# Layer 0 of an encoder trunk: head 3's scores one step later, modulation loaded at three rates, a norm product six tiles wide

## The chip, the cores and the metric

One core of one Trainium2 chip runs the whole kernel in one launch. The metric is the device time of an execution in microseconds. The engines are PE (TensorE: matmuls; its weight loads are shown as PEld), DVE (VectorE), ACT (ScalarE), POOL (GpSimd) and SP (SyncE, which issues the DMAs). SBUF is the memory on the chip from which the engines read; PSUM has eight banks, into which PE writes.

## The reference

A trunk of two layers on 256 tokens of width 2048, in float32. Each layer has two sub-layers, attention and MLP, and each of these is modulated by a conditioning vector `c`:

```python
cond = silu(c)
for l in range(2):
    mod = cond @ w_ada[l] + b_ada[l]                  # 2048 x 12288
    sh_a, sc_a, g_a, sh_m, sc_m, g_m = split(mod, 6)
    h = rmsnorm(x) * (1 + sc_a) + sh_a
    proj = h @ w_in[l]        # dq, dk, dv of 4 differential heads; latent cq, ckv, kr
    out_a = diff_attention(dq, dk, dv, bias)          # softmax(map 0) - lam * softmax(map 1)
    q = rmsnorm(cq) @ w_uq[l]; kv = rmsnorm(ckv) @ w_ukv[l]
    out_b = mla_attention(q, kv, rope(kr))            # 8 latent heads
    x = x + g_a * (concat(out_a, out_b) @ w_o[l])
    h = rmsnorm(x) * (1 + sc_m) + sh_m
    x = x + g_m * (relu(h @ w_mlp_in[l]) ** 2 @ w_mlp_out[l])   # width 8192
return rmsnorm(x) * final_norm_g
```

## The kernel before

**Numbers in two parts.** The weights come from HBM as float32. ACT copies each block to `hi`, which has fewer bits (L144), and DVE makes `lo`, the block less `hi` (L145); the activations are split in the same way. A product is hi x hi + hi x (low activation) + lo x hi. `weights()` does this for one block, 1 MiB as a rule, 0.75 MiB in the norm products. The block lands in a tile `raw`, of which there are five; `hi` and `lo` have four tiles of half a block each, so two blocks' worth.

**Narrow and wide.** `mac` (L177 to L182) issues the three products one by one, each over 256 tokens, and two output tiles share a PSUM bank. `wides` (L191 on) and `wide_by_k` (L248 on) keep a bank for each output tile: the high and the low activations stand side by side, so that one matmul of 512 columns (L201, L258) does the first two products in the two halves of the bank, and one of 256 columns (L204, L260) adds the third. The two halves of the bank have then to be joined: `joined` (an ACT copy, L979, and a DVE add, L980, for each half of a pair of tiles), or `update_wide`, which adds both halves to `x` (L973).

**The modulation.** `w_ada` is 192 blocks of 1 MiB that PE never sees: for each, `ada_load` issues a DMA into one of the five `raw` tiles, and `ada_sums` (L322) has DVE multiply it by `cond` and sum. They are spread over the kernel by credit: every call of `weights()` first queues the sums of what was loaded by the call before, then adds `self.rate` to `self.credit` and issues as many loads as there are whole units in it. `ada_need` forces loads that are wanted at once. The rate before is 0.0 up to the end of layer 0's first norm product, then `RATE_A0` = 1.1 until the MLP's norm product, `RATE_K` = 0.6 in that, and `RATE_M` = 0.66 in the MLP; layer 1 has 0.0, 0.5, 0.7, 0.0 and 0.66. The order of the blocks follows use: shift and scale of the attention's norm, its gate (16 blocks), shift and scale of the MLP's norm (32), the MLP's gate (16), then layer 1.

**The order of a layer** (`layer`, L773). First the norm and the first product; then the rest of `w_d`, the key `w_kr`, and six single columns of `w_t`, with the scores and softmax of the differential heads 0 to 2 (`probs`, `diff_probs`: two maps of two matmuls each, L1036; a DVE reduction, L1037; an exponential on ACT, L1023) between them. Then the latent heads' products up from the latents: keys (`up_k`), four tiles of queries (`up_q(0)`), the rotary part (`up_r`), values (`up_v`), four more tiles of queries (`up_q(1)`), all in PSUM tiles `pss` or `pv`. `probs(3)` stands behind `up_k`. `turn` transposes a head's probabilities. Eight blocks of value weights (`val`, `w_dv`) follow, with the latent heads' scores, transposes and values (`mla`) put between them, then four blocks of `w_oa` (four output tiles by k-quarters) with the differential heads' values (`av`), and twelve tiles of `w_ob` in pairs, each with the update of `x` and its square.

**The MLP's norm product** (`norm_then_by_k`, L660). For each of eight pairs of k-tiles, the normed and modulated pair is made (`modulated`) and multiplied at once, so that the product starts before the norm is through. Six PSUM banks are open. Layer 0 multiplies twelve output tiles narrowly (two to a bank, two weight blocks of 0.75 MiB for each pair), layer 1 six tiles widely (one block for each pair). The tiles of the first 16 that are left, four in layer 0 and ten in layer 1, are made by `wides` in pairs behind it.

The program's own order within an engine is what a scheduler makes of this order when the kernel is built; each engine then works its list from the front.

Of the kernel before, what the change touches and what calls it, by code (L numbers as in the profile page):

```python
# [19 lines left out]
NK = D // P  # L20
# [75 lines left out]
WHOLE = 6  # L96


RATE_A0, RATE_A1, RATE_A2, RATE_K, RATE_K1, RATE_M = 1.1, 0.5, 0.7, 0.6, 0.0, 0.66
FILL = "0|1|2|3||||rlm"  # L100


class Trunk:
# [555 lines left out]

    def norm_then_by_k(self, l, acc, sh, sc, src):  # L660


        r = self.rstd(acc, D, True)
        banks = self.open_banks(6)
        h = []
        for p in range(8):
            k = 2 * p
            for g in (sh, sc):
                self.ada_need(l, g, k + 1)
            new, ins = self.modulated(r, k, self.mod[l, sh], self.mod[l, sc])  # L670
            h += new
            self.hold = None if p else ins
            blocks = self.by_k_weights([src[p, b] for b in range(2 - l)], 6, False)
            if l == 0:
                self.by_k(banks, blocks, h, k, NK, 6)
            else:
                self.wide_by_k(banks, blocks, h, k, NK)
            self.hold = None
        return h, banks

# [92 lines left out]
    def layer(self, l, acc):  # L773
        nc, io = self.nc, self.io
# [15 lines left out]
        if l == 0:  # L790
            early = {p: next_by_k(kqs) for p, kqs in EARLY.items()}
            h, banks = self.first_norm_then_by_k(acc, io["w_a"], 3, fill, early)
        else:
            self.rate = RATE_K1
            h, banks = self.norm_then_by_k(l, acc, 0, 1, io["w_a1"])
        done = sum(len(k) for k in EARLY.values()) if l == 0 else 0
        self.rate = RATE_A0 if l == 0 else RATE_A1
# [25 lines left out]
        def up_k():  # L823
            kn.extend(self.copy(ps, "kn") for ps in self.small(io["w_uk"][l], ckv, 8))

        def up_q(b):
            qn.extend(self.copy(ps, "qn", ms) for ps in self.small(io["w_uq"][l, b], cq, 4))
# [23 lines left out]
        def probs(hd):  # L851
            return lambda: a.append(self.diff_probs(l, hd, q[hd], kk[hd]))
# [28 lines left out]
        if l:  # L881
            self.rate = RATE_A2
        up_k()
        probs(3)()
        up_q(0)
        turn(0)()
        up_r()
        turn(1)()
# [6 lines left out]
        turn(3)()  # L895
        for f in mla[3:6]:
            f()
        self.interleave(
            [val(cg, kq) for cg in range(2) for kq in range(4)],
            mla[6:] + [av[0][0], av[1][0]],  # L900
        )
        acc = None
        g = self.mod[l, 2]
        self.ada_need(l, 2, NK - 1)
        banks = self.open_banks(2)
        self.by_k(banks, self.by_k_weights([io["w_oa"][l, 0]], 4, None), self.mo, 0, NK)
        for f in (av[0][1], av[1][1], av[2][0], av[3][0]):
# [4 lines left out]
        o = self.mo + o  # L912
        for kq in (2, 3):
            self.by_k(banks, self.by_k_weights([io["w_oa"][l, kq]], 4, None), o, 4 * kq, NK)
        for m in range(0, NK, 2):
            if m < 4:
                self.update(m, banks[m // 2], g)
            else:
                self.update_wide(m, self.wides([io["w_ob"][l, m - 4 + j] for j in range(2)], o), g)
            acc = self.sumsq(acc, self.x[:, m : m + 2], m == NK - 2)  # L920

        self.rate = RATE_K1 if l else RATE_K
        h, banks = self.norm_then_by_k(l, acc, 3, 4, io["w_m0"] if l == 0 else io["w_m01"])
        self.rate = RATE_M
        g = self.mod[l, 5]
        acc = None
        late = []
        for fb in range(NFB):
            hid = []
            done = 12 - 6 * l  # L930
            for m in range(0 if fb else done, NK, 2):
                srcs = [io[f"w_m1{l}"][NK * fb + m + j - done] for j in range(2)]
                ps = self.wides(srcs, h)
                if l:
                    banks = [self.joined(banks[i : i + 2], self.t("sum")) for i in range(0, len(banks), 2)]
                for b in banks:
                    hid += self.relu2(b)
                banks = []
                hid += self.relu2(self.joined(ps, self.t("sum")))
            if late:  # L940
                self.ada_need(l, 5, NK - 1)
                for m in range(0, NK, 2):
                    self.update(m, late[m // 2], g)
                late = []
            for m in range(0, NK, 2):
                ps = self.wides([io["w_m2"][l, fb, m + j] for j in range(2)], hid)
                if l == 0 and fb == 0:
# [201 lines left out]
def _layout(i):  # L1149
    f = {k: np.asarray(v) for k, v in i.items()}  # L1150
    a = {}
    a["x"] = np.ascontiguousarray(f["x"][0].reshape(2, P, D))
    a["ck"] = np.ascontiguousarray(f["c"].reshape(NK, P).T)
    pos = f["positions"][0]
    order = [j + 4 * t for j in range(4) for t in range(2)]
    posq = np.tile(pos.reshape(8, 32).T, (4, 1))[:, order]
    a["pos"] = np.ascontiguousarray(np.concatenate([np.broadcast_to(pos, (P, T)), posq], 1))
    a["consts"] = consts()
    feat = lambda v, n: v.reshape(n, P).T
    vec = [feat(f["b_ada"][l], 96) for l in range(2)]  # L1160
    vec += [feat(f["diff_subln_g"][l], 2) for l in range(2)]
    vec += [feat(f["q_norm_g"][l], 4) for l in range(2)]
    vec += [feat(f["kv_norm_g"][l], 2) for l in range(2)]
    vec += [feat(f["final_norm_g"], NK)]
    vec += [np.stack([f[f"diff_lambda_{a}{j}"][l] for a in "qk" for l in range(2) for j in (1, 2)], 1)]
    vec += [np.repeat(f["rel_bias_table"].reshape(8, 4, HD).transpose(1, 0, 2).reshape(4, 32), 32, 0)]
    a["vec"] = np.ascontiguousarray(np.concatenate(vec, 1))
    assert a["vec"].shape == (P, NVEC)
    a["w_ada"] = np.ascontiguousarray(f["w_ada"].transpose(0, 2, 1)).reshape(2, 96, P, D)
    keep = {k: [] for k in ("w_d", "w_t", "w_kr", "w_dv", "w_uq", "w_uk", "w_uv", "w_oa", "w_ob", "w_m2")}  # L1170
    for l in range(2):
        w = f["w_in"][l]
        first = np.concatenate([w[:, 3072:3840], w[:, :768]], 1)
        if l == 0:
            a["w_a"] = np.stack([_kquarters(np.ascontiguousarray(first[:, 768 * j : 768 * j + 768]), 768, 2) for j in range(2)], 1)
        else:
            a["w_a1"] = _kquarters(np.ascontiguousarray(first[:, :768]), 768, 2)[:, None]
            a["w_q1"] = _ktiles(np.ascontiguousarray(first[:, 768:]))
        keep["w_t"].append(_ktiles(np.ascontiguousarray(w[:, 1280:2048])))
        keep["w_d"].append(_kquarters(np.concatenate([w[:, 1024:1280], w[:, 768:1024]], 1)))  # L1180
        keep["w_kr"].append(_ktiles(np.concatenate([w[:, 3840:3904], w[:, 3872:3904], w[:, 3840:3872]], 1))[0])
        keep["w_dv"].append(np.stack([_kquarters(w[:, 2048 + 512 * g : 2560 + 512 * g]) for g in range(2)]))
        w = f["w_uq"][l].reshape(512, HM, 192)
        nope, rope = w[:, :, :128].reshape(512, 1024), w[:, :, 128:].reshape(512, 512)
        keep["w_uq"].append(np.concatenate([_kquarters(np.ascontiguousarray(z)) for z in (nope[:, :512], nope[:, 512:], rope)]))
        w = f["w_ukv"][l].reshape(256, HM, 256)
        keep["w_uk"].append(_kquarters(np.ascontiguousarray(w[:, :, :128]).reshape(256, 1024), 1024, 2)[0])
        keep["w_uv"].append(_kquarters(np.ascontiguousarray(w[:, :, 128:]).reshape(256, 1024), 1024, 2)[0])
        w = np.concatenate([f["w_o"][l][1024:], f["w_o"][l][:1024]])
        keep["w_oa"].append(_kquarters(np.ascontiguousarray(w[:, :512])))  # L1190
        keep["w_ob"].append(_ktiles(np.ascontiguousarray(w[:, 512:])))
        w = f["w_mlp_in"][l]
        if l == 0:
            a["w_m0"] = np.stack([_kquarters(np.ascontiguousarray(w[:, 768 * j : 768 * j + 768]), 768, 2) for j in range(2)], 1)
        else:
            a["w_m01"] = _kquarters(np.ascontiguousarray(w[:, :768]), 768, 2)[:, None]
        a[f"w_m1{l}"] = _ktiles(np.ascontiguousarray(w[:, 1536 - 768 * l :]))
        keep["w_m2"].append(np.stack([_ktiles(f["w_mlp_out"][l][D * b : D * b + D]) for b in range(NFB)]))
    for k, v in keep.items():
        a[k] = np.stack(v)  # L1200
    return a
# [18 lines left out]
```

## Time and profile before

| What | Value |
|---|---|
| Median of three runs | 2212.98 us (2211.97 to 2214.62) |
| The profiled execution's own time | 2212.55 us |
| Its span, first to last instruction | 2210.8 us |
| PE busy | 2180.0 us (99%) |
| DVE busy | 1625.5 us (74%) |
| ACT busy | 1136.4 us (51%) |
| Read from HBM | 581.28 MB, 264 GB/s over the span |
| Mean granted clock of TensorE | 0.997 |

Matmuls are pipelined: one that stands with 0.28 us in a timeline starts 0.12 us behind the one ahead of it. The chain of waits shows these distances. A busy time of PE thus covers short gaps; an idle time is stated in brackets behind a row, with what ended it.

### The profile page before, as it was taken

Reading aid. Unit: us, or ns where it says so; the run is one execution under the profiler, and the core shown is the slowest. Engines: PE = TensorE matmul, PEld = TensorE weight load, DVE = VectorE, ACT = ScalarE, POOL = GpSimd, SP = SyncE. Lnnn points to the kernel's source line nnn. Section 1 sums busy time; section 2 is a strip of 40 time slices with the busy share of each in tenths; the row PEclk is TensorE's granted clock in tenths of the full one; section 3 lists DMA queues with packets and bytes.
Section 4 is the critical chain, followed back from the end, with each engine's and each line's share of the span. In section 5 each row is a group of like instructions: output and inputs, shape, how many; then the busy total and the mean of one; then the engine's idle time right before and its main releaser. Section 6 shows DMA issues by size and latency. Waiting matters only on the chain.

```text
span 2210.8 us, 32403 instructions
## 1 busy us (share of the span) xinstructions
PE 2180.0 (99%) x13010; PEld 1948.1 (88%) x13010; DVE 1625.5 (74%) x2273; ACT 1136.4 (51%) x1691; POOL 1.9 (0%) x10
## 2 busy tenths in 40 slices
PE   7999999999999999999999999999999999999998
PEld 6899888998888888888889988988888888888887
DVE  7899779988878888887886876788655555555555
ACT  6555663465464355355444565546535534534553
POOL 0000000000000000000000000000000000000000
PEclk9999999999999999999999999999999999999999
DMA  9988778888878888888867666677655555555552
GB/s 379 415 348 311 265 269 327 316 328 325 322 305 321 305 323 310 318 324 304 316 218 265 248 229 228 236 263 253 240 189 193 184 189 192 188 183 192 188 189 95
DMA packets 85255, 585.49 MB, mean 265 GB/s; under 512 B 9584, under 2 KB 9968, under 8 KB 19440
## 3 DMA queue, kind: packets, MB, share of 16 engines
q1 hardware_dynamic: 85104, 583.42, 71.1%
q8 instruction: 102, 1.67, 0.3%
q14 instruction: 49, 0.40, 0.0%
HBM read 581.28 MB, written 2.10 MB: 264 GB/s over the span
## 4 chain that ended last, share of the span: by engine, by line
PE 93%; DVE 4%; DMA 2%; ACT 1%; issue 1%; SPq 0%; DVEq 0%; ACTq 0%
PE ps L201 43%; PE ps L204 22%; PE pk L244 3%; PE pk L182 2%; PE pk L181 2%; PE pk L180 2%; PE pk L258 2%; DVE ada L322 2%; PE pv L269 1%; PE pv L270 1%; PE pv L271 1%; DMA ada<-in_w_ada 1%; DVE lo L145 1%; PE pk L260 1%; PE ps L181 1%; PE ps L180 1%
## 5 line engine op out<-in xcount | busy, mean ns | idle before, releaser
L145 DVE TENSOR_TENSOR lo<-raw,hi 128x1024 fp32r<-128x1024 f32 (+1 forms) x714 | 843.0, 1194 | 466.9 <-issue 189.0
L144 ACT ACTIVATE hi<-raw 128x1024 fp32r<-128x1024 f32 (+1 forms) x714 | 731.3, 1035 | 690.6 <-PE ps L201 312.5
L201 PE MATMUL ps<-hid,hi 128*128 128x512 f32 x2048 | 477.5, 390 | 0.0
L322 DVE SCALAR_TENSOR_TENSOR ada<-ada,cond 128x2048 f32<-128x2048 f32 x192 | 438.6, 2286 | 13.6 <-DMA ada<-in_w_ada 13.5
L201 PEld LDWEIGHTS ps<-hid,hi 128*128 128x128 f32 x2048 | 379.7, 188 | 78.1 <-DVE hid L174 1.4
L201 PE MATMUL ps<-h,hi 128*128 128x512 f32 x1856 | 431.7, 390 | 0.0
L201 PEld LDWEIGHTS ps<-h,hi 128*128 128x128 f32 x1856 | 344.7, 188 | 69.2
L204 PEld LDWEIGHTS ps<-hid,lo 128*128 128x128 f32 x2048 | 254.2, 192 | 5.0
L204 PE MATMUL ps<-hid,lo 128*128 128x256 f32 x2048 | 255.7, 283 | 0.0
L204 PEld LDWEIGHTS ps<-h,lo 128*128 128x128 f32 x1856 | 230.3, 192 | 4.5
L204 PE MATMUL ps<-h,lo 128*128 128x256 f32 x1856 | 231.7, 283 | 0.0
L973 DVE SCALAR_TENSOR_TENSOR x<-ps,mod,x 128x256 f32<-128x256 f32 x272 | 124.6, 479 | 6.8 <-PE ps L204 6.6
L979 ACT ACTIVATE sum<-ps 128x256 f32<-128x256 f32 x110 | 42.2, 383 | 115.3 <-PE ps L204 115.1
L182 PE MATMUL pk<-h,lo 128*128 128x256 f32 x320 | 90.4, 283 | 0.0
L181 PE MATMUL pk<-h,hi 128*128 128x256 f32 x320 | 90.4, 283 | 0.0
L180 PE MATMUL pk<-h,hi 128*128 128x256 f32 x320 | 90.1, 285 | 0.0
L244 PE MATMUL pk<-hf,w 128*128 128x256 f32 x384 | 83.9, 379 | 0.0
L244 PEld LDWEIGHTS pk<-hf,w 128*128 128x128 f32 x384 | 72.6, 190 | 10.1 <-ACT hf L614 0.4
L174 DVE TENSOR_TENSOR hid<-relu,hid 128x256 fp32r<-128x256 f32 x128 | 48.3, 422 | 44.8 <-ACT hid L173 44.8
L182 PEld LDWEIGHTS pk<-h,lo 128*128 128x128 f32 x320 | 61.4, 192 | 0.2 <-DVE lo L145 0.2
L181 PEld LDWEIGHTS pk<-h,hi 128*128 128x128 f32 x320 | 61.4, 192 | 0.1
L180 PEld LDWEIGHTS pk<-h,hi 128*128 128x128 f32 x320 | 61.0, 192 | 0.1
(229 smaller groups left out, 2387.0 us busy)
## 6 DMA issues: line engine op xcount, KB each, us to landing
raw<-in_w_m SPq DMA_DIRECT2D x238, 1024.0 KB, 4.8
ada<-in_w_ada SPq DMA_DIRECT2D x192, 1024.0 KB, 4.9
raw<-in_w_ob SPq DMA_DIRECT2D x24, 1024.0 KB, 5.5
raw<-in_w_m SPq DMA_DIRECT2D x24, 768.0 KB, 5.7
raw<-in_w_dv SPq DMA_DIRECT2D x16, 1024.0 KB, 4.8
raw<-in_w_t SPq DMA_DIRECT2D x12, 1024.0 KB, 4.8
w<-in_w_a SPq DMA_DIRECT2D x24, 384.0 KB, 13.8
raw<-in_w_a SPq DMA_DIRECT2D x12, 768.0 KB, 5.4
```

Source lines behind the costliest of these rows:

```text
L144: nc.scalar.activation(hi, v, AF.Copy)
L145: ins = nc.vector.tensor_tensor(lo, v, hi.bitcast(F32), ALU.subtract)
L174: self.nc.vector.tensor_tensor(lo, val[:, i], hi.bitcast(F32), ALU.subtract)
L180: mm(ps, hi, x[0], start=first, stop=False, skip_group_check=shared)
L181: mm(ps, hi, x[1], start=False, stop=False, skip_group_check=shared)
L182: mm(ps, lo, x[0], start=False, stop=last, skip_group_check=shared)
L201: mm(ps.rearrange("p a b -> p (a b)"), part(w, k, 0), x[2], start=k == 0, stop=False)
L204: mm(ps[:, 0], part(w, k, 1), x[0], start=False, stop=k == nk - 1)
L244: self.nc.tensor.matmul(ps, v, whole[k], start=first, stop=last, skip_group_check=True)
L258: mm(ps.rearrange("p a b -> p (a b)"), part(j, 0), both, start=k == 0, stop=False)
L322: ins = nc.vector.scalar_tensor_tensor(w, w, 1.0, self.cond, ALU.mult, ALU.mult, accum_out=acc[:, i : i + 1])
L973: self.nc.vector.scalar_tensor_tensor(x, ps[i][:, j], g[:, m + i : m + i + 1], x, ALU.mult, ALU.add)
```

## The change

Three things. `probs(3)`, in both layers, comes behind `up_q(0)`. In layer 0 the rate becomes 1.75 with the value blocks (`RATE_V0`), 2.0 with `w_oa` (`RATE_O0`), 1.0 with `w_ob` (`RATE_T0`), and 0.0 in the MLP's norm product. And that product is made as in layer 1: six tiles wide, with the ten others behind it in pairs. The weights are laid out in memory to match.

```diff
-RATE_A0, RATE_A1, RATE_A2, RATE_K, RATE_K1, RATE_M = 1.1, 0.5, 0.7, 0.6, 0.0, 0.66
+RATE_A0, RATE_V0, RATE_O0, RATE_T0, RATE_A1, RATE_A2, RATE_M = 1.1, 1.75, 2.0, 1.0, 0.5, 0.7, 0.66
...
     def norm_then_by_k(self, l, acc, sh, sc, src):
...
-            blocks = self.by_k_weights([src[p, b] for b in range(2 - l)], 6, False)
-            if l == 0:
-                self.by_k(banks, blocks, h, k, NK, 6)
-            else:
-                self.wide_by_k(banks, blocks, h, k, NK)
+            self.wide_by_k(banks, self.by_k_weights([src[p]], 6, False), h, k, NK)
...
         up_k()
+        up_q(0)
         probs(3)()
-        up_q(0)
         turn(0)()
...
+        if l == 0:
+            self.rate = RATE_V0
         self.interleave(
             [val(cg, kq) for cg in range(2) for kq in range(4)],
             mla[6:] + [av[0][0], av[1][0]],
...
         self.ada_need(l, 2, NK - 1)
+        if l == 0:
+            self.rate = RATE_O0
         banks = self.open_banks(2)
...
+        if l == 0:
+            self.rate = RATE_T0
         for m in range(0, NK, 2):
             if m < 4:
                 self.update(m, banks[m // 2], g)
...
-        self.rate = RATE_K1 if l else RATE_K
-        h, banks = self.norm_then_by_k(l, acc, 3, 4, io["w_m0"] if l == 0 else io["w_m01"])
+        self.rate = 0.0
+        h, banks = self.norm_then_by_k(l, acc, 3, 4, io["w_m0"][l])
         self.rate = RATE_M
...
-            done = 12 - 6 * l
-            for m in range(0 if fb else done, NK, 2):
-                srcs = [io[f"w_m1{l}"][NK * fb + m + j - done] for j in range(2)]
+            for m in range(0 if fb else 6, NK, 2):
+                srcs = [io["w_m1"][l, NK * fb + m + j - 6] for j in range(2)]
                 ps = self.wides(srcs, h)
-                if l:
+                if banks:
                     banks = [self.joined(banks[i : i + 2], self.t("sum")) for i in range(0, len(banks), 2)]
```

More of the change, by code (lines that the diff above doesn't have):

```diff
@@ L793, in layer @@
         else:
-            self.rate = RATE_K1
+            self.rate = 0.0
             h, banks = self.norm_then_by_k(l, acc, 0, 1, io["w_a1"])
@@ L920, in layer @@
             acc = self.sumsq(acc, self.x[:, m : m + 2], m == NK - 2)
-        self.rate = RATE_K1 if l else RATE_K
-        h, banks = self.norm_then_by_k(l, acc, 3, 4, io["w_m0"] if l == 0 else io["w_m01"])
+        self.rate = 0.0
+        h, banks = self.norm_then_by_k(l, acc, 3, 4, io["w_m0"][l])
         self.rate = RATE_M
@@ L1169, in _layout @@
     a["w_ada"] = np.ascontiguousarray(f["w_ada"].transpose(0, 2, 1)).reshape(2, 96, P, D)
-    keep = {k: [] for k in ("w_d", "w_t", "w_kr", "w_dv", "w_uq", "w_uk", "w_uv", "w_oa", "w_ob", "w_m2")}
+    keep = {k: [] for k in ("w_d", "w_t", "w_kr", "w_dv", "w_uq", "w_uk", "w_uv", "w_oa", "w_ob", "w_m0", "w_m1", "w_m2")}
     for l in range(2):
@@ L1176, in _layout @@
         else:
-            a["w_a1"] = _kquarters(np.ascontiguousarray(first[:, :768]), 768, 2)[:, None]
+            a["w_a1"] = _kquarters(np.ascontiguousarray(first[:, :768]), 768, 2)
             a["w_q1"] = _ktiles(np.ascontiguousarray(first[:, 768:]))
@@ L1192, in _layout @@
         w = f["w_mlp_in"][l]
[L1193 to L1197, printed above, removed]
+        keep["w_m0"].append(_kquarters(np.ascontiguousarray(w[:, :768]), 768, 2))
+        keep["w_m1"].append(_ktiles(np.ascontiguousarray(w[:, 768:])))
         keep["w_m2"].append(np.stack([_ktiles(f["w_mlp_out"][l][D * b : D * b + D]) for b in range(NFB)]))
```

## The prediction

> **What bounds the kernel now.** I read the page first, then busy time by stretch, then the chain and the timelines at the places that the change touches.
>
> ```profile
> span 2210.8 us, 32403 instructions
> PE 2180.0 (99%) x13010; PEld 1948.1 (88%) x13010; DVE 1625.5 (74%) x2273; ACT 1136.4 (51%) x1691; POOL 1.9 (0%) x10
> PE 93%; DVE 4%; DMA 2%; ACT 1%; issue 1%; SPq 0%; DVEq 0%; ACTq 0%
> ```
>
> TensorE is 93% of the chain that ended last. Time can therefore come from three places only: fewer or cheaper matmuls, the few waits on the other 7%, and the clock.
>
> ```profile
> 149.20:206.50 57.30, 55.52 (x441) 54.35 (x439) 54.14 (x102) 33.44 (x58) 0.00 (x0) 1.00 0.85 320
> 206.50:242.00 35.50, 34.60 (x220) 30.91 (x221) 29.10 (x52) 22.84 (x45) 0.00 (x0) 0.95 0.72 267
> 242.00:305.00 63.00, 63.00 (x292) 52.19 (x291) 45.99 (x72) 35.11 (x70) 0.00 (x0) 1.00 0.74 275
> 305.00:337.10 32.10, 32.10 (x241) 30.62 (x240) 22.77 (x33) 20.45 (x47) 0.00 (x0) 1.00 0.64 235
> 337.10:407.70 70.60, 68.02 (x387) 59.33 (x387) 65.62 (x85) 27.26 (x31) 0.00 (x0) 1.00 0.90 332
> 414.90:484.20 69.30, 69.30 (x578) 69.25 (x578) 63.37 (x88) 34.82 (x52) 0.00 (x0) 1.00 0.90 328
> 484.20:595.30 111.10, 111.10 (x641) 98.18 (x640) 92.16 (x122) 59.46 (x87) 0.00 (x0) 1.00 0.84 314
> 1411.80:1479.00 67.20, 66.86 (x386) 59.02 (x384) 56.09 (x75) 29.14 (x33) 0.00 (x0) 1.00 0.78 286
> 1486.50:1520.20 33.70, 33.70 (x193) 29.58 (x194) 27.81 (x45) 19.60 (x30) 0.00 (x0) 1.00 0.62 214
> 1520.20:1631.40 111.20, 111.20 (x641) 98.28 (x641) 74.07 (x101) 60.78 (x89) 0.00 (x0) 1.00 0.64 233
> ```
>
> Columns: the stretch, its length, then busy time of PE, PEld, DVE, ACT and POOL, granted clock, DMA share, GB/s. In order these are, for layer 0: the remaining columns of the input projection with the first up-projection, the other up-projections, the value products with the latent heads, the first part of the output projection (`w_oa`), its second part (`w_ob`), the MLP's norm product, and ten pairs of its MLP. Then for layer 1: `w_ob`, the norm product, ten MLP pairs. Two things stand out. The output projection's second part takes 70.60 us in layer 0 and 67.20 in layer 1 for the same matmuls, with DVE at 65.62 of 70.60. And one stretch has a clock of 0.95.
>
> **The norm product: narrow to wide, and its six other tiles.** Before, layer 0 multiplies twelve output tiles by each of 16 k-tiles in three narrow matmuls; after, six tiles are made wide (one of 512 columns and one of 256), and the other six go to the pairs behind, which are wide already.
>
> ```profile
> 418.10 0.12 PE pk L182
> ...
> 484.22 7.28 PE ps L201 x32
> 491.50 3.83 PE ps L204 x32
> ```
>
> Narrow: 3 x 0.12 = 0.360 us for a tile and k-tile. Wide: 7.28/32 + 3.83/32 = 0.2275 + 0.1197 = 0.347. There are 12 x 16 = 192 such products: 192 x 0.0128 = 2.5 us less. By stretches: 69.30 us go; in their place come layer 1's 33.70 for six tiles and three pairs of 7.28 + 3.83 = 11.11, together 67.0: **2.3 us less**, which I take. Layer 1's norm product runs without the modulation's loads, as layer 0's will. The wide form adds three joins, each twice an ACT copy and a DVE add:
>
> ```profile
> L979 ACT ACTIVATE sum<-ps 128x256 f32<-128x256 f32 x110 | 42.2, 383 | 115.3 <-PE ps L204 115.1
> ...
> L980 DVE SCALAR_TENSOR_TENSOR sum<-ps,sum 128x256 f32<-128x256 f32 x110 | 46.0, 419 | 0.3 <-ACT sum L979 0.3
> ```
>
> A join is 2 x (0.383 + 0.419) = 1.6 us, and it lies beside the next pair's matmuls: layer 1 has these joins, and its ten pairs took 111.20 against layer 0's 111.10, so 0.1 at most. If that cover were gone, the three would cost up to 4.8. Bounds: 2.5 less to 2.5 more.
>
> The Trainium skill, TensorE: Matmul & The Clock Gate, Back-to-back issue gap, puts an isolated warm gap at N/2.4 + 2.5 ns. An estimate from it: 3 x 109.2 = 327 ns narrow, 215.8 + 109.2 = 325 wide, a gain of 0.5 us in place of 2.5; the 0.12 and 0.2275 us of the chain disagree with it and decide.
>
> **Head 3's scores behind the latent queries' product.** The code moves them in both layers. In layer 0 they are where the clock fell (below: PE's timeline, ACT's, DVE's, then busy time by microsecond):
>
> ```profile
> 202.95 0.28 PE L182 MATMUL pss<-lath,lo 128*128 128x256 f32 x1
> 204.59 1.13 PE L1036 MATMUL psc<-k,q 128*128 128x256 f32 x4 [1.36 <-ACT k L288]
> ...
> 206.55 1.18 PE L1036 MATMUL psc<-k,q 128*128 128x256 f32 x2 [0.46 <-DVE mx L1037]
> ...
> 202.51 0.51 ACT L1023 ACTIVATE s<-s,mx 128x256 f32<-128x256 f32 x1 [1.89 <-DVE mx L1037]
> ...
> 203.02 1.04 ACT L144 ACTIVATE hi<-raw 128x1024 fp32r<-128x1024 f32 x1
> 203.97 0.57 ACT L288 ACTIVATE k<-ps 128x512 f32<-128x512 f32 x1
> ...
> 198.30 1.22 DVE L145 TENSOR_TENSOR lo<-raw,hi 128x1024 fp32r<-128x1024 f32 x1
> ...
> 207.00:208.00 1.00, 1.00 (x5) 0.82 (x5) 0.23 (x1) 0.19 (x2) 0.00 (x0) 0.50 0.00 0
> 209.00:210.00 1.00, 1.00 (x7) 1.00 (x6) 0.55 (x4) 1.00 (x2) 0.00 (x0) 0.50 0.00 0
> 210.00:211.00 1.00, 1.00 (x9) 0.94 (x8) 1.00 (x1) 0.28 (x2) 0.00 (x0) 0.98 0.00 0
> ```
>
> The first score matmul waits for head 3's key, whose copy on ACT stands behind head 2's exponential and a weight split; PE sits idle 1.36 us, and 0.46 more for a bank. Just behind, the clock is at 0.50 for some 3.4 us (0.95 over 35.5 us is a loss of 1.8): half of that is lost, 1.7 us. Together 3.5 us. After the change 48 narrow matmuls (5.8 us) of the queries' product stand there; counting blocks in the order of their loads, the `lo` that ends at 199.5 is the last of their weights, and the key's copy ends at 204.5, before these 5.8 us (from 203.1) are over. I take **3.5 us less**. Bounds: nothing, if the exponentials and reductions, pushed back behind other DVE work, make a later matmul wait as long; 1 us of loss, if only the idle part returns where the backlog has grown; 4 us of gain. In layer 1 the same matmuls follow without idle time, so nothing is won there:
>
> ```profile
> 1281.64 0.28 PE L182 MATMUL pss<-lath,lo 128*128 128x256 f32 x1
> 1281.76 1.03 PE L1036 MATMUL psc<-k,q 128*128 128x256 f32 x4
> ```
>
> The Trainium skill, TensorE: Matmul & The Clock Gate, Part 1: The HAM clock gate, says the clock is gated in free-running windows of 3413 ns by how busy PE was; the rows agree in the length, and by that rule the 1.7 us go whole or not at all.
>
> **The modulation's loads, moved.** A load of 1 MiB and a DVE sum belong together. Credit per weight block: 13 blocks at 1.1 make 14 loads in both. Then before 9 for the 8 value blocks, 4 for `w_oa`, 13 for `w_ob`, 10 for the 16 norm blocks; after 14 (1.75), 8 (2.0), 12 (1.0) and 0. So 10 go from the norm, which was never short of weights (PE 69.30 of 69.30), and 8 more are in by the projection's end. The two that are left over go to the MLP, where DVE has 92.16 of 111.10: no cost. The 48 loads are just the 16 of the gate and the 32 that the MLP's norm needs, so none has to be forced there.
>
> ```profile
> L322 DVE SCALAR_TENSOR_TENSOR ada<-ada,cond 128x2048 f32<-128x2048 f32 x9 | 20.6, 2285 | 0.0
> L145 DVE TENSOR_TENSOR lo<-raw,hi 128x1024 fp32r<-128x1024 f32 x16 | 19.6, 1223 | 11.7 <-ACT hi L144 11.7
> ...
> L145 DVE TENSOR_TENSOR lo<-raw,hi 128x1024 fp32r<-128x1024 f32 x8 | 9.8, 1224 | 9.6 <-ACT hi L144 9.6
> L322 DVE SCALAR_TENSOR_TENSOR ada<-ada,cond 128x2048 f32<-128x2048 f32 x4 | 9.1, 2283 | 0.0
> ```
>
> First two rows: value stretch; last two: `w_oa`. Sums trail their loads by one block, so 4 more run in each: 4 x 2.37 (2.285 and the accumulator's read) = 9.5 us. The value stretch comes to 55.5 of 63.0, where DVE idled 11.7 ahead of `lo`; `w_oa` to 32.3 of 32.1, where it idled 9.6: just full. Queued behind each sum on DVE are the next block's `lo` and the heads' small steps, for which PE waits. DVE was as full (54 of 57 us) from 149.2 to 206.5, and PE lost there little but the wait above; in `w_ob`, at 65.62 of 70.60, it lost 70.60 - 67.20 = 3.4. Between 0 and 3.4 I take **1.0 more** for both stretches.
>
> For `w_ob` I take **no change**: 13 sums by the count before (two blocks early, one double among them) and 13 after (two from the last `w_oa` block). The double moves from its middle to its head. Bounds: 3.4 less (layer 1's time) to 3.4 more.
>
> **Sum.** -2.3 - 3.5 + 1.0 = -4.8. The profiled execution took 2212.55 us, span 2210.8 and 1.75 around it; 2207.7 follows. The median of the runs is 2212.98, 0.4 above; 0.2% of it, about what a measurement can tell from no change, is 4.4 us, so the border to "faster" is 2208.6.
>
> **Rivals.** *The ring of five buffers becomes the bound (slower).* Weights and modulation loads share five tiles. With one load per block, a weight load goes out when the block two before has been split; with two per block, by counting the tiles through the program, seven loads of the twelve value and `w_oa` blocks and the first of `w_ob` go out only behind the block just before.
>
> ```profile
> raw<-in_w_ob SPq DMA_DIRECT2D x12, 1024.0 KB, 6.2
> raw<-in_w_dv SPq DMA_DIRECT2D x8, 1024.0 KB, 4.8
> raw<-in_w_oa SPq DMA_DIRECT2D x4, 1024.0 KB, 5.2
> ...
> 387.45 7.64 DMA raw<-in_w_ob
> 395.19 1.06 ACT hi L144
> ```
>
> Loop: landing + two `hi` of 1.06 + the last `lo` of 1.22. At 4.8 it is 8.1 us, at 5.2 8.5, at 6.2 9.5, at 7.64 11.0; PE needs 32.1/4 = 8.0 a block. At 5.2 seven loops are late by 3.5 us, which the one block in advance (8 us) covers. At 6.2 they are late by 10.5; if the stock is used up already, the result is 2212.55 - 5.8 + 10.5 = 2217.3. At 7.64 it is 21 less 8 in stock: 2219.7. It decides from a median landing of about 6 us. For it: the last two rows, where PE waited for just such a load. Against it: spaced like this, three transfers per 8 us leave the weight load almost alone, as in the value stretch's 4.8.
>
> *The DMA engines are the bound.* The new stretches need 22 MiB in 63.0 us (366 GB/s) and 12 MiB in 32.1 (392).
>
> ```profile
> GB/s 379 415 348 311 265 269 327 316 328 325 322 305 321 305 323 310 318 324 304 316 218 265 248 229 228 236 263 253 240 189 193 184 189 192 188 183 192 188 189 95
> ```
>
> The second slice moved 415, above both. At a limit of 358 they would take 64.4 and 35.1, that is 4.4 more than now in place of 1.0: 2211.2. The Trainium skill, DMA: Bandwidth & Descriptors, Specifications, gives that 358 as a core's share of HBM; the slice of 415 speaks against it, and I give it little.
>
> *The scores' stall only moves.* DVE's backlog stays, PE waits as long elsewhere: -2.3 + 1.0, 2211.3.
>
> *`w_ob` runs free too.* Without a double in its middle it goes like layer 1's: 3.4 less again, 2204.3.
>
> **How the numbers follow.** Forecast 0.50 (2205 to 2210.5: 0.37 faster, 0.13 same), `w_ob` free 0.20 (faster), stall moves 0.15 (same), DMA bound 0.03 (same), ring 0.12 (0.10 slower, 0.02 same). Faster 0.57, same 0.33, slower 0.10. The range from 2203 to 2215.5 takes in the first four; the ring and a gain beyond 2203 stay out.
>
> **What would show it.** Right: no stretch at clock 0.50 near 206 us; the norm product in 33 to 34 us, followed by pairs at 11.11; PE without idle time over 0.5 us in the value blocks and `w_oa`, DVE there at 55 and 32 us; landings of their weights at about 5 us. Wrong: `hi` waiting for `in_w_dv` or `in_w_oa` landings, PE idle ahead of `pv` or `pk`; a second fall of the clock; psc matmuls waiting at a new place.

## Result and profile after

Slower: 2228.88 us, median of four runs, against 2212.94 of the kernel before on the same chip; ratio 1.0076 (95% interval 1.0063 to 1.0088), 14 to 19 us. The forecast was 2207.7, with 2203.0 to 2215.5 as its range. The profiled execution took 2228.57 us. First the page, then busy time by stretch (length; PE, PEld, DVE, ACT, POOL; granted clock; DMA share; GB/s), with the stretches set at the same events as in the prediction.

```profile
span 2226.8 us, 32020 instructions
PE 2185.3 (98%) x12818; PEld 1942.2 (87%) x12818; DVE 1629.8 (73%) x2281; ACT 1140.7 (51%) x1699; POOL 1.9 (0%) x10
```

```profile
196.90:217.30 20.40, 20.40 (x162) 19.83 (x160) 17.15 (x36) 12.37 (x26) 0.00 (x0) 1.00 0.77 281
217.30:233.30 16.00, 10.01 (x24) 6.40 (x24) 13.70 (x24) 5.53 (x11) 0.00 (x0) 0.68 0.83 316
249.20:310.20 61.00, 61.00 (x283) 50.53 (x282) 48.92 (x78) 30.81 (x62) 0.00 (x0) 1.00 0.86 322
313.30:348.10 34.80, 30.14 (x230) 28.74 (x228) 29.43 (x44) 19.74 (x45) 0.00 (x0) 1.00 0.90 347
348.10:418.30 70.20, 69.41 (x386) 60.55 (x387) 69.00 (x83) 28.78 (x33) 0.00 (x0) 0.98 0.91 344
426.60:460.30 33.70, 33.69 (x193) 29.60 (x194) 27.80 (x46) 19.46 (x30) 0.00 (x0) 1.00 0.67 230
460.30:571.50 111.20, 111.20 (x642) 98.28 (x641) 89.08 (x118) 63.95 (x98) 0.00 (x0) 1.00 0.79 300
```

Three readings. In the first row TensorE works without a gap where it had stood still before. The second row shows the price, right behind it: 10.01 of 16.00 us busy, at a mean clock of 0.68. The value blocks (third row) are gapless, `w_oa` (fourth) is not, and the norm product (sixth) is what was forecast. The fifth and seventh rows are `w_ob` and ten pairs of the MLP. TensorE's timeline has the idle time and what ended it:

```profile
221.10 3.78 PE L1009 MATMUL pqr<-qr,K 128*128 128x512 f32 x4 [3.78 <-ACT qr L288]
...
229.51 0.81 PE L1103 MATMUL psm<-kr,qr 128*128 128x256 f32 x2 [2.21 <-DVE qr L1014]
...
348.13 2.31 PE L201 MATMUL ps<-mo,hi 128*128 128x512 f32 x7 [3.62 <-ACT hi L144]
...
1308.61 3.62 PE L1009 MATMUL pqr<-qr,K 128*128 128x512 f32 x4 [2.77 <-ACT qr L288]
...
1314.67 0.67 PE L1103 MATMUL psm<-kr,qr 128*128 128x256 f32 x2 [1.57 <-DVE qr L1014]
```

Two waits in each layer, before the rotary product (`pqr`) and before the latent heads' first rotary scores (`psm`), and one at `w_ob`'s first product. In the first four the product waits for a copy or a step that is queued behind something else on ACT or DVE; the one at `w_ob` waits for weights that landed late (below). DVE's own timeline of the first place (start, length):

```profile
209.88 0.42 DVE L1037 CUSTOM_DVE_ANT_0 s<-psc,bias 128x256 f32<-128x256 f32 x1 [0.28 <-PE psc L1036]
...
210.23 2.29 DVE L322 SCALAR_TENSOR_TENSOR ada<-ada,cond 128x2048 f32<-128x2048 f32 x1
...
212.44 0.42 DVE L1037 CUSTOM_DVE_ANT_0 s<-psc,bias 128x256 f32<-128x256 f32 x1
...
212.86 2.28 DVE L322 SCALAR_TENSOR_TENSOR ada<-ada,cond 128x2048 f32<-128x2048 f32 x1
...
215.15 0.40 DVE L1037 CUSTOM_DVE_ANT_0 s<-psc,bias 128x256 f32<-128x256 f32 x1
...
217.12 0.42 DVE L1037 CUSTOM_DVE_ANT_0 s<-psc,bias 128x256 f32<-128x256 f32 x1 [0.42 <-PE psc L1036]
```

Head 3's four reductions start 2.6, 2.7 and 2.0 us apart, because a modulation sum of 2.28 us (in the last interval a `lo`) stands in each. ACT takes the exponentials one by one behind them and, after the last, two weight splits and the transposed probabilities, before it copies the rotary queries:

```profile
217.59 0.51 ACT L1023 ACTIVATE s<-s,mx 128x256 f32<-128x256 f32 x1 [1.33 <-DVE mx L1037]
...
218.10 1.99 ACT L144 ACTIVATE hi<-raw 128x1024 fp32r<-128x1024 f32 x2
...
220.47 1.07 ACT L288 ACTIVATE qr<-pss 128x512 f32<-128x512 f32 x2
```

The up-products end at 217.3; the copy that `pqr` needs starts at 220.47. From there the chain of waits runs on DVE (start, length, what):

```profile
217.12 0.42 DVE s L1037
...
218.76 2.20 DVE ada L322 x2
...
223.62 1.14 DVE lo L145
224.75 2.21 DVE ada L322 x2
...
229.51 0.81 PE psm L1103 x2
```

4.4 of these 12.4 us are two more sums. No DMA stands in this chain from 210 to 250 us, so late weights are not what TensorE waited for here. In layer 1 one sum stands among the reductions, which are 1.5, 2.6 and 1.4 us apart, and one ahead of the rotary step (the rope, L1012 to L1014).

### The profile page after: what moved, and what is told of

Its sections match the earlier page's. It is cut to its first block, busy times and chain, and to the rows that moved or that the text cites. A ratio compares the mean times of both kernels' runs of the same rounds, so it can differ in the third digit from the quotient of the medians.

```text
span 2226.8 us, 32020 instructions
## 1 busy us (share of the span) xinstructions
PE 2185.3 (98%) x12818; PEld 1942.2 (87%) x12818; DVE 1629.8 (73%) x2281; ACT 1140.7 (51%) x1699; POOL 1.9 (0%) x10
## 4 chain that ended last, share of the span: by engine, by line
PE 92%; DVE 5%; DMA 1%; ACT 1%; issue 1%; SPq 0%; DVEq 0%; ACTq 0%
PE ps L201 43%; PE ps L204 22%; PE pk L244 3%; PE pk L258 3%; DVE ada L322 2%; DVE lo L145 2%; PE pk L260 2%; PE pv L271 1%; PE pv L269 1%; PE pv L270 1%; PE pk L182 1%; PE pk L181 1%; PE pk L180 1%; PE ps L181 1%; PE ps L182 1%; PE ps L180 1%
## 5 line engine op out<-in xcount | busy, mean ns | idle before, releaser
L201 PE MATMUL ps<-h,hi 128*128 128x512 f32 x1952 | 454.0, 390 | 0.0
L322 DVE SCALAR_TENSOR_TENSOR ada<-ada,cond 128x2048 f32<-128x2048 f32 x192 | 438.3, 2285 | 13.6 <-DMA ada<-in_w_ada 13.5
L201 PEld LDWEIGHTS ps<-h,hi 128*128 128x128 f32 x1952 | 362.5, 188 | 72.8
L204 PEld LDWEIGHTS ps<-h,lo 128*128 128x128 f32 x1952 | 242.3, 192 | 4.7
L204 PE MATMUL ps<-h,lo 128*128 128x256 f32 x1952 | 243.7, 283 | 0.0
L258 PE MATMUL pk<-h,hi 128*128 128x512 f32 x288 | 74.8, 395 | 0.2
L258 PEld LDWEIGHTS pk<-h,hi 128*128 128x128 f32 x288 | 50.9, 189 | 9.3 <-issue 0.4
L985 ACT ACTIVATE relu<-sum 128x512 f32<-128x512 f32 x64 | 40.1, 628 | 36.3 <-DVE sum L980 36.3
L182 PE MATMUL ps<-h,lo 128*128 128x256 f32 x192 | 55.5, 289 | 0.0
L180 PE MATMUL ps<-h,hi 128*128 128x256 f32 x192 | 55.5, 289 | 0.0
L181 PE MATMUL ps<-h,hi 128*128 128x256 f32 x192 | 55.0, 287 | 0.0
```

Source lines behind the costliest of these rows:

```text
L180: mm(ps, hi, x[0], start=first, stop=False, skip_group_check=shared)
L181: mm(ps, hi, x[1], start=False, stop=False, skip_group_check=shared)
L182: mm(ps, lo, x[0], start=False, stop=last, skip_group_check=shared)
L201: mm(ps.rearrange("p a b -> p (a b)"), part(w, k, 0), x[2], start=k == 0, stop=False)
L204: mm(ps[:, 0], part(w, k, 1), x[0], start=False, stop=k == nk - 1)
L258: mm(ps.rearrange("p a b -> p (a b)"), part(j, 0), both, start=k == 0, stop=False)
```

## The experiments

Each ratio is against runs of the kernel before on the same chip (medians 2211.17, 2211.84 and 2211.41 us for e1 to e4, e5 to e8, e9 to e12). These medians and the changed kernel's own 2212.94 differ by up to 1.8 us, so differences across the groups are taken between the distances from them.

**Which of the three parts.** e1 is the changed kernel with head 3's scores back ahead of `up_q(0)`; e2 is the kernel before with the scores' move alone; e3 is the kernel before with the four new rates alone (its norm product narrow, at rate 0.0).

```diff
 e1, against the kernel after
         up_k()
+        probs(3)()
         up_q(0)
-        probs(3)()
 e2, against the kernel before
         up_k()
-        probs(3)()
         up_q(0)
+        probs(3)()
 e3, against the kernel before, each where the change has it
+        if l == 0: self.rate = 1.75     # value blocks
+        if l == 0: self.rate = 2.0      # w_oa
+        if l == 0: self.rate = 1.0      # w_ob
-        self.rate = RATE_K1 if l else RATE_K
+        self.rate = 0.0                 # norm product
```

> The changed kernel with head 3's scores put back ahead of the latent queries' product; rates and the wide norm product stay. Theory A (the scores' move costs about 6.2 us in each layer, the rates about 5.8 between the value blocks and the norm, the wide product wins 2.3): 2228.9 - 12.4 = 2216.5 us; layer 1 as in the kernel before. Theory B (the rates fill DVE, and the stall at the rotary product is only a sequel of that): 2226 to 2229, the time stays lost.

> The kernel before with only the scores moved behind the latent queries' product, in both layers. Theory A: 2212.9 + 12.4 = 2225.3 us, PE idle ahead of the rotary matmul in both layers and the clock at half behind it. Theory B: 2209.4 to 2213, as the prediction had it, since the rates are those of before.

> The kernel before with only the rates changed: 1.75, 2.0, 1.0 and 0.0 in the (narrow) norm product. Theory A: 2212.9 + 5.8 = 2218.7 us, PE waiting for the first weights of the output projection's second part, about 4 us, with a clock at half behind it. Theory B: 2226 or more. If the prediction's term was right: 2214.

Measured: e1 2215.52 (1.0022, interval 1.0012 to 1.0031), e2 2224.74 (1.0063, 1.0048 to 1.0078), e3 2217.40 (1.0027, 1.0016 to 1.0037). The scores' move costs 13.6 us, in both layers (in the changed kernel the value blocks of layer 0 start at 249.2 in place of 243.0 us, and layer 1 needs 29.1 us from the first up-product to the first latent value product, in place of 22.4), the rates 6.2, and the wide norm product, e1 less e3, wins 1.9; together 17.9, within the 14 to 19 of the whole change. From the other side, the whole change (15.9) less e1 (4.4), the scores' move is 11.6. Theory A's forecasts were near in all three, theory B's in none. e2's timeline of PE has both waits of layer 0 without any of the new rates:

```profile
220.30 3.04 PE L1009 MATMUL pqr<-qr,K 128*128 128x512 f32 x4 [3.78 <-ACT qr L288]
...
228.71 1.19 PE L1103 MATMUL psm<-kr,qr 128*128 128x256 f32 x2 [3.18 <-DVE qr L1014]
```

So the rates did not make this stall.

**Later still.** e4 puts `probs(3)` behind `up_r` and `turn(1)`, so that the rotary copy is ahead of the exponentials on ACT.

```diff
         up_k()
-        probs(3)()
         up_q(0)
         turn(0)()
         up_r()
         turn(1)()
+        probs(3)()
         mla[0]()
```

> The kernel before with head 3's scores two products later, behind the rotary part, ahead of the first latent head. Theory A with the queue on ACT as its mechanism (head 3's exponentials stand ahead of the rotary copies for which PE waits): no such wait now, layer 0's old stall of 3.5 us gone, layer 1 as before: 2209.4 us. Rival within A (DVE and ACT simply have too much there, any later place makes PE wait): 2218 to 2225.

2222.69 (1.0056, 1.0041 to 1.0071). The rival within A is what came. The wait ahead of `pqr` is gone, so head 3's steps ahead of the copy did make that one; but the stall turns up at the latent heads' softmax:

```profile
232.32 1.22 PE L1102 MATMUL psm<-kn,qn 128*128 128x256 f32 x2 [3.98 <-DVE sm L1104]
...
237.74 1.22 PE L1102 MATMUL psm<-kn,qn 128*128 128x256 f32 x2 [3.34 <-DVE sm L1104]
```

Head 3's reductions are 3.2, 1.6 and 2.6 us apart there: the chain is as long as before and stands ahead of the next softmax.

**The sums among the reductions.** e5 is e2 without a modulation load from `up_k` to `up_q(1)`, with those loads made up in the value blocks; e9 has the same rates and the scores in their old place.

```diff
+        self.rate = 0.0
         up_k()
         up_q(0)
         probs(3)()
...
+        self.rate = RATE_A2 if l else 1.75      # value blocks
...
+        if l == 0:
+            self.rate = RATE_A0                 # from w_oa on
```

> The scores moved as in e2 (2224.7 there), but no modulation load and so no 2.3 us sum on VectorE from the key up-product to the second query up-product, in both layers; the loads left out there are made up in the value blocks (1.75 a block in layer 0). Theory C (the sums between head 3's four reductions stretch its softmax, and the stalls before the rotary product and before the latent scores come of that): the stalls of 3.9 and 3.4 us in layer 0 shrink to under 1 us each and their half clock goes, layer 1's 2.9 and 2.0 us too; the value blocks start at or before 243 us of the span, and the time is 2209 to 2213 (no more than 0.1% over before). Rival (four softmax steps behind the last up-product but one don't fit into what is left of the matmuls, with sums or without): the two stalls stay above 2 us each and the time is 2219 or more (at least 0.3% over before).

> The kernel before with e5's rates (no modulation sums from the key up-product to the second query up-product, 1.75 a block in layer 0's value blocks), and head 3's scores in their old place: the control to e5 (2208.9), which differs from it by the scores' place alone. Theory C (it is the sums among the reductions that make the stalls in either order): the old order's wait of 1.5 and 0.6 us in layer 0 and its 3.4 us at half clock go as well, and the time is 2207.5 to 2210.5, level with e5 within 0.1%. Rival (my forecast's reading: in the old order the scores have nothing in front of them and TensorE waits whatever VectorE does, so that the place itself is worth 3.5 us): 2212 to 2213.5.

e5: 2208.94 (0.9989, 0.9980 to 0.9999). e9: 2211.50 (1.0000, 0.9990 to 1.0009). Leaving the sums out is worth nothing in the old order and some 16 us in the new one (e2's 2224.7 to 2208.9). In e5's timeline of DVE (its L1039 is the kernel's L1037) the reductions are 1.5, 1.2 and 1.3 us apart, and TensorE goes from the up-products into the rotary product without a wait:

```profile
210.33 0.42 DVE L1039 CUSTOM_DVE_ANT_0 s<-psc,bias 128x256 f32<-128x256 f32 x1
...
211.81 0.42 DVE L1039 CUSTOM_DVE_ANT_0 s<-psc,bias 128x256 f32<-128x256 f32 x1
...
212.99 0.40 DVE L1039 CUSTOM_DVE_ANT_0 s<-psc,bias 128x256 f32<-128x256 f32 x1
...
214.25 0.42 DVE L1039 CUSTOM_DVE_ANT_0 s<-psc,bias 128x256 f32<-128x256 f32 x1 [0.85 <-PE psc L1038]
```

```profile
216.91 1.97 PE L1011 MATMUL pqr<-qr,K 128*128 128x512 f32 x4
...
220.75 0.59 PE L1105 MATMUL psm<-kr,qr 128*128 128x256 f32 x2
```

The four records of `pqr` take 1.97 us here and 3.78 in the changed kernel: there they ran at the half clock. (The profile shows each float32 matmul as two records, so these are two matmuls.) e9 fell between its two expectations: its old wait was shorter but still there (`psc` waited 1.16 us for the key's copy, in place of 1.36), and it met a half-clock window of 3.4 us in `w_ob` that e5 did not. By the medians the move by itself, e9 to e5, is worth about 2.5 us where no sums stand in its way, but the intervals of the two overlap. In the traces 1.6 us of it has been won when layer 0's value blocks start (238.32 against 240.02, from up-products that start at 196.32 and 196.38), and 1.7 is e9's half-clock window in `w_ob`, which is not the move's doing.

**The half clock.** e6 is the changed kernel with 17 matmuls that compute nothing ahead of the rotary product (34 records in the profile).

```diff
         def up_r():
             raw = [self.copy(ps, "qr", ms) for ps in self.small(io["w_uq"][l, 2], cq, 4)]
+            self.warm(self.cond, 17)
             qr.extend(self.rope_q(x) for x in raw)
```

> The changed kernel with 17 extra matmuls that compute nothing (128 columns, about 0.21 us each by the steps of the transposes at full clock, 3.6 us in all) between the rotary queries' up-product and the rotary product, in both layers, so that TensorE has work in the idle stretch there (3.8 us in layer 0, 2.8 us in layer 1). Theory D (the granted clock of 0.5 from 219.7 to 226.5 us costs time of its own, half of 6.8 us): 2225 to 2226. Rival E (VectorE, which works without a gap from 217.1 to 229.4 us, sets the end of this stretch, and the half clock of TensorE is covered by it): 2227.5 to 2230, no change within 1.5 us, with the second stall ahead of the latent scores as long as it is or longer.

2222.63 (1.0053, 1.0037 to 1.0069): 10.8 us over the kernel before where the changed kernel is 15.9 over, so 5.1 us less, by adding work. e6's timeline of PE, then the stretches from the up-products' end on (layer 0, layer 1) in e6 and in the changed kernel:

```profile
216.39 3.96 PE L599 MATMUL pw<-cond,ident 128*128 128x128 f32 x34
220.34 1.98 PE L1010 MATMUL pqr<-qr,K 128*128 128x512 f32 x4
...
228.75 0.80 PE L1104 MATMUL psm<-kr,qr 128*128 128x256 f32 x2 [2.34 <-DVE qr L1015]
```

```profile
216.40:233.00 16.60, 14.26 (x72) 11.31 (x71) 14.41 (x25) 7.29 (x13) 0.00 (x0) 0.90 0.78 306
1302.00:1312.00 10.00, 9.35 (x57) 7.45 (x56) 9.79 (x17) 4.22 (x9) 0.00 (x0) 1.00 0.69 246
```

```profile
217.30:234.00 16.70, 10.71 (x27) 7.02 (x27) 13.70 (x24) 5.74 (x11) 0.00 (x0) 0.69 0.80 303
1305.80:1317.00 11.20, 6.86 (x22) 3.89 (x21) 10.38 (x19) 4.44 (x10) 0.00 (x0) 0.85 0.69 247
```

Mean clock 0.90 in place of 0.69 and 1.00 in place of 0.85: of the 10.2 us at 0.5 in layer 0 one window of 3.4 is left, behind the second wait. From the latent products' start to the latent values in layer 1 it took 26.0 us (1281.9 to 1307.9) in place of 29.1 (1285.9 to 1315.0); in layer 0, from the first up-product to the value blocks, 50.4 in place of 52.3. These two are 5.0 us. In the traces a further 2.1 are in e6's `w_oa` with the wait behind it, where the fillers do nothing: that wait was 2.74 us in place of 3.62, and no window at 0.5 followed it. Both expectations were right in part: the wait for `qr` on DVE stayed (2.34 us, up to 12.4 us behind the up-products' end, where the changed kernel has 12.2), as E said, but at full clock TensorE does more of its other work around it, and the gain was larger than D's. The Trainium skill, TensorE: Matmul & The Clock Gate, Part 1: The HAM clock gate, has windows of 3413 ns gated by how busy PE was; the windows at 0.5 in these runs were 3.4, 6.8 and 10.2 us long, which agrees, and filling one wait took whole windows away.

**The rates: ring or VectorE.** e7 is e1 with 1.5 in place of 2.0 in `w_oa` and 1.17 in place of 1.0 in `w_ob`; e8 is e1 with six `raw` buffers.

```diff
 e7
-RATE_A0, RATE_V0, RATE_O0, RATE_T0, ... = 1.1, 1.75, 2.0, 1.0, ...
+RATE_A0, RATE_V0, RATE_O0, RATE_T0, ... = 1.1, 1.75, 1.5, 1.17, ...
 e8
-        self.up = pool("up", 40)
+        self.up = pool("up", 37)
-        raw = self.wp.tile([P, width], F32, tag="raw", name=self.name("raw"), bufs=5)
+        raw = self.wp.tile([P, width], F32, tag="raw", name=self.name("raw"), bufs=6)
```

> e1 (changed kernel with the scores in their old place, 2215.5) with 1.5 modulation loads a block in w_oa in place of 2.0, and 1.17 in place of 1.0 in w_ob, which brings the same number by the norm. Theory F (at two loads a block each weight load takes the raw buffer of the block just before, so the first load of w_ob is issued too late and TensorE waits 2.8 us for it and then runs 3.4 us at half clock): the wait ahead of w_ob's first product shrinks to under 1 us and the time is 2210 to 2212.5. Rival G (VectorE is full in w_oa and w_ob together, 65 of 68 us busy, and the sums have to be done somewhere): the wait moves into w_ob and the time stays at 2214.5 to 2217.

> e1 (2215.5) with six raw buffers in place of five (paid for with 37 in place of 40 tiles of the pool for the up-products). Theory F (the ring of raw buffers issues w_ob's first load too late): with a sixth, that load is issued one block earlier, the wait of 2.8 us ahead of w_ob's first product goes, and the time is 2210 to 2212.5. Rival G (VectorE's total work): the wait stays above 1.5 us there or turns up in w_ob, 2214.5 to 2217.

e7 2215.04 (1.0014, 1.0004 to 1.0024), e8 2215.06 (1.0017, 1.0007 to 1.0026): neither is clear of e1's 2215.52, by the intervals. They failed for different reasons. `w_oa` and `w_ob` together, by stretch, in the kernel before, e1, e7 and e8:

```profile
307.20:409.30 102.10, 99.52 (x630) 89.67 (x629) 88.49 (x117) 46.37 (x74) 0.00 (x0) 1.00 0.83 304
```

```profile
307.10:411.50 104.40, 100.89 (x630) 90.97 (x629) 98.36 (x126) 49.17 (x77) 0.00 (x0) 0.98 0.92 346
```

```profile
306.60:414.60 108.00, 102.69 (x632) 91.86 (x630) 100.32 (x130) 48.68 (x77) 0.00 (x0) 0.97 0.91 343
```

```profile
310.00:411.40 101.40, 100.87 (x636) 90.55 (x634) 97.07 (x123) 48.56 (x79) 0.00 (x0) 1.00 0.91 340
```

e7 is as G said: the waits moved into `w_ob`. In e8 the stretch is shorter than before the change, with 9 us more on DVE, and the clock stays at 1.00. Issues on SP, e1 then e8:

```profile
332.37 0.33 SPq L156 DMA_DIRECT2D raw<-in_w_ob x1
```

```profile
328.65 0.33 SPq L156 DMA_DIRECT2D raw<-in_w_ob x1
```

The sixth buffer lets `w_ob`'s first load go 12.1 us ahead of the end of `w_oa`'s matmuls (340.7), where e1 has 4.7 (337.1). So F's mechanism held in this stretch. What was won there, e8 lost ahead of it (its value blocks start at 246.8 us, e1's at 242.9): with one more tile the sums came earlier, and two of them, at 208.2 and 210.8 us, stood ahead of head 3's first two reductions in their old place (in e1 none ran from 202.1 to 211.4). A score matmul then waited 3.07 us for its bank:

```profile
210.91 0.70 PE L1036 MATMUL psc<-k,q 128*128 128x256 f32 x2 [3.07 <-DVE mx L1037]
```

**All parts together.** e10 is the changed kernel with e5's pause and four other rates in layer 0; e11 adds e8's sixth buffer; e12 is e11 with other rates again.

```diff
 e10, e11: value blocks, w_oa, w_ob, norm product
-RATE_V0, RATE_O0, RATE_T0 = 1.75, 2.0, 1.0              # and 0.0
+RATE_V0, RATE_O0, RATE_T0, RATE_N0 = 2.0, 1.5, 1.1, 0.66
 e12
+RATE_V0, RATE_O0, RATE_T0, RATE_N0 = 2.0, 2.0, 1.0, 0.0
 all three
+        self.rate = 0.0
         up_k()
```

> The changed kernel (scores behind, norm product six tiles wide) with other rates: none from the key up-product to the second query up-product in both layers, then in layer 0 2.0 a block in the value blocks, 1.5 in w_oa, 1.1 in w_ob, 0.66 in the norm product, which brings all by the norm's end. By theory C the stalls of the scores' move are gone (e5: 2208.9) and the norm product gives 1.9 to 2.4 us; what is open is whether the loads packed into the value blocks and w_oa make w_ob's first load late again (e3: 2.8 us and 1.7 us of half clock). Without that 2206 to 2208, faster than before by 0.2 to 0.3%; with it 2210 to 2213.

> e10 with six raw buffers in place of five (37 tiles in place of 40 in the up-products' pool). In e8 the sixth took the 2.8 us ahead of w_ob away, and what it won was lost where one more sum fell among head 3's reductions; here no sums stand there. By that reading: as fast as e10 or up to 4.5 us faster, by the size of e10's wait ahead of w_ob; 2204 to 2208. Rival (VectorE's total, not the ring, sets w_ob): within 1 us of e10.

> The changed kernel with all three of its parts kept, and what the experiments point to: six raw buffers (37 tiles in the up-products' pool), no modulation sums from the key up-product to the second query up-product in both layers, then 2.0 loads a block in layer 0's value blocks and in w_oa, 1.0 in w_ob, none in the norm product. Worked out from e5, e8 and e1: w_oa starts at 302.7 us of the span as in e5 and e11, w_oa and w_ob together take 101.4 as in e8, so the norm product is reached at 404 to 405, and from there it is 721 to layer 1's first norm as in e8; with e5's layer 1 the span is 2204 and the time 2206 to 2209, faster than before by 0.1 to 0.2%. Rival (VectorE and the DMA queues are full: VectorE was busy 97.1 of 102.4 us in e11's w_oa and w_ob): w_ob's stalls grow by what the two loads more a block bring, and the time is 2211 to 2215.

e10 2219.11 (1.0034, 1.0023 to 1.0045), e11 2214.24 (1.0011, 1.0002 to 1.0020), e12 2213.29 (1.0006, 0.9997 to 1.0015). None repeats e5, and none came within its first forecast (2206 to 2208, 2204 to 2208, 2206 to 2209); for e12 its rival's 2211 to 2215 did. e10 and e11 pay in the norm product, which makes its activations on DVE just ahead of PE and can't carry sums at 33.70 us as it did at 69.30; the waits of PE from 417 to 453 us in e10 are these:

```profile
PE pk L258 <- DVE h L641: 5.4, 6, 1.7
```

e12 keeps the norm product free, and the wait at `w_ob`'s first product is back, with six buffers:

```profile
336.42 1.80 PE L201 MATMUL ps<-mo,hi 128*128 128x512 f32 x5 [2.49 <-ACT hi L144]
```

The loads that the norm product gives up are not what costs this by themselves: e8 carried them through `w_oa` and `w_ob` with 43.42 us of sums and lost nothing there (101.40 us in place of 102.10). e12 has the loads of the pause to make up as well, 46.67 us of sums in these two. That this is what brings its wait is a reading of the two traces; no run separates it. Of all kernels here e5 is the fastest: the scores' move, the narrow norm product, and a pause of the sums. It is 0.1% faster than before, with an interval that just leaves out no change.

## Why the prediction was wrong

**The scores' term failed, in size and in sign.** Forecast: 3.5 us less, bounds 4 less to 1 more, and nothing in layer 1. Measured: 13.6 more (e2), from both layers. The first half of the step came true: the three up-products now run through in 20.40 us, the wait at `psc` and the clock's fall near 206 us are gone, and the key's copy is in time. The step that failed is the reading that the key's readiness makes the moved scores free, and with it the bound of "1 us of loss, if only the idle part returns where the backlog has grown". It took the stall for a thing that is moved with its size. What the runs showed is a chain: four reductions on DVE, each with its exponential on ACT, that stretch when 2.28 us sums fall between them (e5: 1.2 to 1.5 us apart; the changed kernel: 2.0 to 2.7). In the old place two up-products stand behind the scores, `up_q(0)` and `up_r`; in the new place only `up_r`, and e4, with neither, has the stall at yet another place. That the matmuls are the chain's cover is read from these three, not measured by itself. The prediction counted which copy would be ready for the moved matmuls, and not what stands behind their results on ACT and DVE: the rotary copy, the rope, and the latent heads' first softmax. It had named a place as a doubt ("psc matmuls waiting at a new place"), but the ones that waited were other matmuls, not `psc`. Its rival "the scores' stall only moves" (0.15) had the mechanism, DVE's backlog and a wait elsewhere, and mis-sized it: it priced the waits at what they were before, 1.8 us and a window; they were 3.78 and 2.21 us in layer 0 and 2.77 and 1.57 in layer 1.

**That layer 1 had no idle time did not make it safe.** It did not mean that there was cover to spare: 4.3 us of waits (2.77 and 1.57) came up at the same two places.

**The clock, a second-order term, was left out of the loss.** The half-clock window was in the forecast only as a gain. Each new wait of 2 to 4 us brought windows at 0.5 of its own: 6.8 us from 219.7, 3.4 from 229.9, 3.4 from 349.4, 3.4 from 1308.5, 17 us in all; an estimate from that is a loss of up to half, 8.5 us, if TensorE has work throughout. In e6 only one of 3.4 us is left in these places, and it is 5.1 us faster.

**The loads' term was mis-sized.** 1.0 more was forecast for the value blocks and `w_oa`, and 0 for `w_ob`; e3 measured 6.2 (interval 3.5 to 8.2). For TensorE the value blocks were right: 61.00 of 61.00. DVE was not as full as forecast in the two stretches, 48.92 and 29.43 us in place of 55 and 32. The loss that the traces show came at one point, `w_ob`'s first product, by the rival of the ring, at its end only: 2.65 us of wait in e3 with a window at 0.5 of 3.4 us behind it, 3.62 and 3.4 in the changed kernel (which has 1.07 more inside `w_oa`). e3's profiled execution was its fastest, 2215.92 us, and is 3.7 us behind when the norm product starts; where the rest of the 6.2 lies, no trace shows. The chain of waits of the changed kernel there:

```profile
331.62 4.79 DMA raw<-in_w_oa
...
336.43 1.07 ACT hi L144
...
337.53 2.37 DVE lo L145 x2
...
339.92 7.08 DMA raw<-in_w_ob
```

This is the rival's loop, landing, `hi`, `lo`, next landing, with one long landing of 7.08 us in it. Its price was put at 10 to 21 us less the stock because seven loops were thought late at landings of 6.2 to 7.64 us; the landings of `w_oa` took 4.8 us (its row among the changed kernel's DMA issues), and just the last loop was late:

```profile
raw<-in_w_oa SPq DMA_DIRECT2D x4, 1024.0 KB, 4.8
```

"`w_ob` no change" held for the stretch's length, 70.20 us in place of 70.60; the term counted the sums and not that the double at its head delays the first load, and the clock's window behind it was not in it. That the ring sets this wait is shown by e8, where a sixth buffer took it away, for its rates; e12 has a wait of 2.49 us there with six buffers and more loads.

**The norm product was right.** 33.70 us, and pairs at 11.12 us: 2.3 less by stretches, 1.9 by medians. By the medians this term alone can't be told from nothing (e1's interval and e3's overlap).

**The DMA engines were no bound in the value blocks.** TensorE had no gap there at 322 GB/s, and none in e12's at 356 (238.85 to 302.77 us). For `w_oa`, with 347, the runs leave it open whether shared engines stretched the one landing of 7.08 us.

## What to carry to other kernels

A step that is moved later takes its whole chain along: count what stands behind its results on each engine's queue, and which matmuls are still left to cover it, before its first operand's readiness is counted as a gain. Long filler instructions (here sums of 2.28 us) that are free beside a steady stream are not free between the links of a chain that several engines pass back and forth; it paid to stop them for the length of the chain, which turned 13.6 us of loss into 2.9 of gain (e2, e5; the gain's interval ends just short of nothing). And where TensorE stops for 2 to 4 us, price the clock's window that can follow the stop with it.

## What the runs showed of the hardware

Work that computes nothing was worth about 5 us: 17 matmuls in a wait of 3.8 us kept the granted clock at 1.00 there, where without them it was at 0.5 for 6.8 us.

Waits of one length do not all bring a window. e9 had one of 2.70 us in `w_ob`, and 3.4 us at 0.5 followed; e5 had one of 2.71, e6 one of 2.74 and e11 one of 2.97, and the clock stayed at 1.00. The traces show what differed. (A step is here one of 3.413 us.) Within an execution the stretches at 0.5 begin whole multiples of 3.413 us apart: in the changed kernel at 35.35, 219.67, 229.91, 349.38 and 1308.52 us, which are 54, 3, 35 and 281 such steps. Cut into these steps from 40 us on, the traces show the clock at 0.5 behind every step in which TensorE, at full clock, was busy with its products for 1.45 us or less, and not behind one with 1.80 us or more; between 1.58 and 1.70 us both came. e9's wait fell nearly whole into one step, which was left with 1.00 us of work. e5's lay across two, with 1.69 and 2.43, e6's with 2.19 and 1.89, e11's with 1.89 and 1.96. Busy time is not all of it: beside the norm, whose matmuls have one column, the clock fell with more (e9 near 2201 us, behind 2.32). This is read from the traces; no run moved a wait in order to test it. By it, whether a kernel loses another 1.7 us behind a wait of some 2.7 us is in part luck.
